# A Trainium2 encoder block: stacked parts in the low-rank factors, head norms on VectorE, and attention tables made inside the first feed-forward

## The chip, the core and the metric

The kernel runs on one core of a Trainium2 chip. That core has four compute engines with their own instruction queues: TensorE (PE, matrix products into PSUM), VectorE (DVE), ScalarE (ACT) and GpSimd (POOL). SyncE (SP) only issues DMAs, as ACT and POOL also can. Each engine works through its queue in order and waits on semaphores for the others. The metric is the device time of one execution in microseconds (us); lower is better.

## What is computed

Two layers on x of shape (1, 512, 1024), float32: an RWKV-7 time mixing with a SwiGLU feed-forward, then a differential attention with another. The parts that the change touches:

```
w = -softplus(-(w0 + tanh(xw @ w1) @ w2)) - 0.5        # w1: 1024x64, w2: 64x1024
a = sigmoid(a0 + (xa @ a1) @ a2)                       # a1: 1024x64, a2: 64x1024
g = sigmoid(xg @ g1) @ g2                              # g1: 1024x160, g2: 160x1024
...
y = (y - mean) * rsqrt(var + 64e-5)                    # per head of 64
y = y * lnx_w + lnx_b
y = y + sum(r * k * r_k) * v
x = x + (y * g) @ w_o
...
q = partial_rope(rms_norm(q, q_norm_g))                # likewise k, with k_norm_g
lam = exp(sum(lam_q1 * lam_k1)) - exp(sum(lam_q2 * lam_k2)) + lam_init
```

## The kernel before

Activations lie transposed: 1024 features as eight tiles of 128 partitions by 512 tokens. A product is kept near float32 by splitting both sides into a high part (a cast to fp32r, on ACT) and a low part (the rest, a subtraction on DVE) and adding three fp32r products (`mm3`, L156 to L158): high by high, low activation by high weight, high activation by low weight. The low-rank factors are the exception: `lora` and `lora2` (L384, L400) use plain fp32 tiles.

The RWKV layer comes first, to about 526 us. Its 16 heads are worked in two halves, w = 0 and 1. `lora` for w1 and a1 runs beside the first half of r; `rates` then makes w2 and a2 into the sigmoids for a half (four output tiles each, L400 with the sigmoid L493 as evacuation, four PSUM banks `pj`). Behind that `plan` merges three streams in an order fixed by the due times in `TIMES`: half 0 (`pairs`, `solve`, the recurrence `rec`), half 1 the same, and a stream of projections that ends with `gate` (the first factor g1, a sigmoid) and `out_half(0)`. `out_half` calls `lora2` with the two pieces of g2 (128 and 32 rows) and multiplies each result by the heads' output (evacuations L597, L601, L603), then projects with w_o, whose high and low parts are made at L617 and L618. `out_half(1)` comes after everything else, at the tail of the layer.

`head_out` normalizes one tile of 128 tokens and eight heads: mean and variance on DVE (L839 to L846, the square L843 on ACT), then `rsqrt`, whose first step is a power on POOL (L227) with three small DVE steps behind it (L229 to L231), the multiplication L853 on DVE, for each parity of heads the gain (L857) and the bonus times v (L858) on POOL, the sum L860 on DVE, and four transpositions on PE (L865), copied out on ACT (L866). It runs eight times, four for each half. `rsqrt_v` (L239 to L245) is a version that stays on DVE, used for the norms of the pairs.

The first feed-forward follows to 895 us, then the attention to 1166 us and the second feed-forward. Each begins with a norm of its input, `norm_cols`: squares on ACT (L267), their sums on POOL and DVE (L272, L274), a product with ones on PE (L281), then L283, the power L227 and L229 to L231; in the feed-forward also L253 and, on PE, L254. The attention's setup makes its tables there: a broadcast load of 192 KB (`lv`, L928) from ACT's queue, rotary tables with the norm gains (L935 to L945, DVE), and lambda (L947 to L951, with an exponential on ACT). The feed-forward's weights come through `load_w`: DMA, cast `wh` (L150, ACT), low part `wl` (L151, DVE). The gain tiles of the norm are `xa` and `xb` (L296 on ACT, L297 on DVE). The order of each engine's queue follows from the order of the code and from when buffers come free, as a scheduler decides it.

## Time and profile before

| | |
|---|---|
| median of three runs | 1536.3 us (1527.12 to 1544.98) |
| the profiled execution | 1535.6 us |
| its span, first to last instruction | 1533.8 us |
| PE busy | 1461.6 us, 95% |
| DVE, ACT, POOL busy | 766.8, 521.4, 210.7 us |

The span is what the rows' times count from; 1.8 us of the execution lie around it. A share of busy time is an average over stages with different limits. A row in the timeline names in brackets how long the engine was idle before it and what ended that. In the windows view the granted clock of TensorE is given as a share of the full 2.4 GHz; 0.50 is 1.2 GHz.

### The profile page before, as it was taken

How to read it: one execution, taken by the hardware profiler on the slowest of the kernel's cores; microseconds unless marked ns; L12 is line 12 of the kernel's file. 1: busy time of each engine (PE TensorE's matmuls, PEld its weight loads, DVE VectorE, ACT ScalarE, POOL GpSimd, SP SyncE). 2: the span in 40 equal slices, each digit the busy share in tenths (PEclk: the TensorE clock that was granted, in tenths of full speed). 3: DMA queues.
4: the chain of work that ended last, by engine and by line, in shares of the span. 5: the costliest groups of instructions: out<-in, count | busy, mean ns of one | idle time of the engine just before them, and what ended most of it. 6: DMA issues, size and time to landing. Idle time of an engine off the chain costs nothing.

```text
span 1533.8 us, 23005 instructions
## 1 busy us (share of the span) xinstructions
PE 1461.6 (95%) x9576; PEld 1133.6 (74%) x9576; DVE 766.8 (50%) x1420; ACT 521.4 (34%) x913; POOL 210.7 (14%) x180
## 2 busy tenths in 40 slices
PE   3899998999998999999999989999999999999999
PEld 2475655766585778888888879998778888888887
DVE  6645558586354644343423276666666444443222
ACT  4552241213212432222222153456654332222111
POOL 0013212112022111111100013211001111111000
PEclk9999999999699899999999999999999999999999
DMA  4022434756131222222222231211012222222231
GB/s 143 18 100 98 154 113 139 279 208 206 61 107 46 97 96 95 95 87 96 95 97 96 96 107 65 83 56 56 29 42 97 97 96 96 97 96 96 98 124 67
DMA packets 51801, 154.24 MB, mean 101 GB/s; under 512 B 5488, under 2 KB 12016, under 8 KB 49648
## 3 DMA queue, kind: packets, MB, share of 16 engines
q1 hardware_dynamic: 50496, 151.18, 28.8%
q8 instruction: 75, 1.23, 0.3%
q10 hardware_dynamic: 1120, 1.32, 0.3%
q14 instruction: 30, 0.25, 0.1%
q0 software_dynamic: 80, 0.26, 0.0%
HBM read 131.77 MB, written 20.97 MB: 100 GB/s over the span
## 4 chain that ended last, share of the span: by engine, by line
PE 82%; DVE 8%; ACT 3%; POOL 3%; issue 2%; DMA 1%; ACTq 0%; SPq 0%; POOLq 0%; DVEq 0%
PE pj L156 15%; PE pj L157 14%; PE pj L158 14%; PE pj L182 3%; PE pj L216 3%; PE d L1007 3%; PE d L1009 2%; PE d L1008 2%; PE cb L698 2%; PE ca L788 2%; PE cb L830 2%; POOL ty L227 2%; PE pj L400 2%; PE a L1105 1%; PE ca L158 1%
## 5 line engine op out<-in xcount | busy, mean ns | idle before, releaser
L150 ACT CAST wh<-wr 128x1024 fp32r<-128x1024 f32 x153 | 161.0, 1053 | 498.3 <-PE pj L157 224.4
L151 DVE TENSOR_TENSOR wl<-wr,wh 128x1024 fp32r<-128x1024 f32 x153 | 187.0, 1223 | 184.2 <-ACT wh L150 182.6
L156 PE MATMUL pj<-xa,wh 128*128 128x512 f32 x352 | 139.2, 395 | 1.3 <-ACT wh L150 1.3
L157 PE MATMUL pj<-xa,wh 128*128 128x512 f32 x352 | 138.9, 395 | 0.0
L158 PE MATMUL pj<-xa,wl 128*128 128x512 f32 x352 | 138.8, 395 | 0.0
L156 PE MATMUL pj<-xb,wh 128*128 128x512 f32 x352 | 137.1, 389 | 0.0
L158 PE MATMUL pj<-xb,wl 128*128 128x512 f32 x352 | 137.1, 389 | 0.0
L157 PE MATMUL pj<-xb,wh 128*128 128x512 f32 x352 | 136.9, 389 | 0.0
L897 POOL TENSOR_TENSOR hid<-ev,hid 128x512 fp32r<-128x512 f32 x44 | 68.2, 1549 | 403.6 <-ACT hid L896 403.6
L893 DVE TENSOR_TENSOR ev<-pj,bc 128x512 f32<-128x512 f32 x44 | 30.4, 691 | 144.1 <-PE pj L158 144.1
L227 POOL TENSOR_TENSOR ty<-ty,mhalf 128x8 f32<-128x8 f32 (+1 forms) x28 | 49.1, 1752 | 302.4 <-DVE ty L846 148.8
L890 DVE TENSOR_TENSOR ev<-pj,bc 128x512 f32<-128x512 f32 x44 | 30.4, 692 | 117.6 <-PE pj L158 115.0
L156 PEld LDWEIGHTS pj<-xa,wh 128*128 128x128 f32 x352 | 66.3, 188 | 17.4 <-ACT wh L150 2.2
L157 PEld LDWEIGHTS pj<-xa,wh 128*128 128x128 f32 x352 | 66.3, 188 | 15.5
L158 PEld LDWEIGHTS pj<-xa,wl 128*128 128x128 f32 x352 | 66.3, 188 | 15.5
L157 PEld LDWEIGHTS pj<-xb,wh 128*128 128x128 f32 x352 | 66.1, 188 | 13.8
L156 PEld LDWEIGHTS pj<-xb,wh 128*128 128x128 f32 x352 | 66.1, 188 | 13.6
L158 PEld LDWEIGHTS pj<-xb,wl 128*128 128x128 f32 x352 | 66.1, 188 | 13.6
L158 PE MATMUL pj<-hid,wl 128*128 128x512 f32 x176 | 68.5, 389 | 0.0
L156 PE MATMUL pj<-hid,wh 128*128 128x512 f32 x176 | 68.5, 389 | 0.0
L157 PE MATMUL pj<-hid,wh 128*128 128x512 f32 x176 | 68.5, 389 | 0.0
L216 PE MATMUL pj<-wr,xk 128*128 128x512 f32 x128 | 61.8, 622 | 0.0
(310 smaller groups left out, 3095.4 us busy)
## 6 DMA issues: line engine op xcount, KB each, us to landing
wr<-in_wgu SPq DMA_DIRECT2D x88, 512.0 KB, 3.5
wr<-in_wdn SPq DMA_DIRECT2D x44, 512.0 KB, 3.5
st_d<-z SPq DMA_DIRECT2D x16, 1024.0 KB, 4.7
z<-st_d SPq DMA_DIRECT2D x16, 1024.0 KB, 5.8
wr<-in_w_kv SPq DMA_DIRECT2D x16, 512.0 KB, 3.5
wr<-in_w_r SPq DMA_DIRECT2D x8, 512.0 KB, 3.4
wr<-in_w_k SPq DMA_DIRECT2D x8, 512.0 KB, 3.5
wr<-in_w_v SPq DMA_DIRECT2D x8, 512.0 KB, 3.5
```

The lines of the kernel that those rows point to most:

```text
L150: nc.scalar.copy(hi, raw)
L151: nc.vector.tensor_tensor(out=lo, in0=raw, in1=hi.bitcast(F32), op=ALU.subtract)
L156: mm(out, wh, xh, start=start, stop=False)
L157: mm(out, wh, xl, start=False, stop=False)
L158: mm(out, wl, xh, start=False, stop=stop)
L182: self.nc.tensor.matmul(pss[i], w[:, kt % 2, i * P:i * P + P], x, start=kt == kts[0], stop=kt == kts[-1])
L216: self.nc.tensor.matmul(pss[tt], x[:, tt * P:(tt + 1) * P], w[:, kt % 2, :], start=kt == 0, stop=kt == KT - 1)
L227: nc.gpsimd.tensor_tensor(out=y, in0=m, in1=half.to_broadcast(shp), op=ALU.pow)
L400: self.nc.tensor.matmul(ps, a[:, i * P:i * P + P], t[0:r], start=n == 0, stop=n == len(ws) - 1)
L698: nc.tensor.matmul(ps[f, o:o + P], BK[f, hf * 4 + c2 * 2 + c, u, :], Z[f, c2 * 2 + c, 0:2, :].rearrange("p a b -> p (a b)"), start=True, s ...
L897: nc.gpsimd.tensor_tensor(out=t[:, 1, :], in0=b, in1=t[:, 0, :].bitcast(F32), op=ALU.subtract)
L1007: mm(ps[:, t], x[:, 0, :], hi, start=kt == 0, stop=False)
```

## The change

Four things change.

1. The second low-rank factors are computed with fp32r products instead of fp32 ones. For w2 and a2 the weight is loaded twice, one copy under the other (128 rows), the activation is stored as its high part in rows 0 to 63 and its low part in rows 64 to 127, and one product of 128 rows does two of the three terms; a second, of 64 rows with the low weight, does the third. For this the first factor's weights are loaded side by side twice (`repeat`), so that its result comes out twice. For g2 the 128-row piece is split as elsewhere, and the 32-row piece is stacked three times (96 rows), so that each output takes four products.
2. In `head_out` the inverse root is `rsqrt_v` on DVE, the gain is multiplied on DVE, and the bonus multiplication on POOL is written ahead of the root.
3. The attention's tables move out of `attn` into `attn_setup`, called at the seventh column of the first feed-forward; `lv` and `lp` get a buffer of their own.
4. The first gate factor's last part gets 96 rows instead of 32.

```diff
@@ -53,12 +53,12 @@
...
-    LO = dict(rk="p", dc="p", z0="p", ka="p", bk="p", yf="d", yl="p", vt="p", su="d", sv="d")
-    AT = dict(lv=1, ah=2, al=2, kq=8, e=3, pt=2, hq=7, hu=2, sq=2, jk=1, h8=4)
+    LO = dict(rk="p", dc="p", z0="p", ka="p", bk="p", yf="d", yl="d", vt="p", su="d", sv="d")
+    AT = dict(ah=2, al=2, kq=8, e=3, pt=2, hq=7, hu=2, sq=2, jk=1, h8=4)
...
@@ -336,7 +336,7 @@
...
-                self.open(st, "hl", dict(wh=2, wl=2), reuse_waits="tile")
+                self.open(st, "hl", dict(wh=2, wl=2, lv=1, lp=1), reuse_waits="tile")
                 x = self.ffn(x, 0, "xa")
...
@@ -373,31 +373,66 @@
...
-    def lora(self, h, m, W1, act, dst, tag):
-        nc = self.nc
-        ws = [self.load_raw(w, [P, KT, w.shape[2]]) for w in W1]
+    def repeat(self, src, n):
+        r = src.shape[2]
+        t = self.T("wr", [P, KT, n * r])
+        for i in range(n):
+            self.nc.sync.dma_start(t[:, :, i * r:i * r + r], src)
+        return t
+    def lora(self, h, m, W1, out, tag):
+        nc = self.nc
+        ws = [self.repeat(w, n) for w, n in W1]
         pss = [self.bank(tag) for _ in W1]
         for kt in range(KT):
             x = self.mix_tile(h, m, kt)
             for ps, w in zip(pss, ws):
                 nc.tensor.matmul(ps[0:w.shape[-1], :], w[:, kt, :], x, start=kt == 0, stop=kt == KT - 1)
             yield
-        for w, ps, t in zip(ws, pss, dst()):
-            r = w.shape[-1]
-            if act is None:
-                nc.vector.tensor_copy(t[0:r], ps[0:r, :])
-            else:
-                nc.scalar.activation(t[0:r], ps[0:r, :], act)
-    def lora2(self, parts, W2, w, evac):
-        ws = [self.load_raw(a[:, w * 512:w * 512 + 512], [a.shape[0], 512]) for a in W2]
+        out(*pss)
+    def halves(self, dst, src):
+        nc = self.nc
+        nc.scalar.copy(dst, src)
+        nc.vector.tensor_tensor(out=dst[C:P], in0=src[C:P], in1=dst[C:P].bitcast(F32), op=ALU.subtract)
+    def lora2(self, x, W2, w, evac):
+        nc = self.nc
+        raw = self.T("wr", [P, 512])
+        for f in (slice(0, C), slice(C, P)):
+            nc.sync.dma_start(raw[f], W2[:, w * 512:w * 512 + 512])
+        hi, lo = self.T("ho", [P, 512], F32R), self.T("ho", [P, 512], F32R)
+        nc.scalar.copy(hi, raw)
+        nc.vector.tensor_tensor(out=lo[0:C], in0=raw[0:C], in1=hi[0:C].bitcast(F32), op=ALU.subtract)
         for i in range(4):
             ps = self.bank()
-            for n, (t, a) in enumerate(zip(parts, ws)):
-                r = a.shape[0]
-                self.nc.tensor.matmul(ps, a[:, i * P:i * P + P], t[0:r], start=n == 0, stop=n == len(ws) - 1)
+            c = slice(i * P, i * P + P)
+            nc.tensor.matmul(ps, hi[:, c], x, start=True, stop=False)
+            nc.tensor.matmul(ps, lo[0:C, c], x[0:C], start=False, stop=True)
+            evac(w * 4 + i, ps)
+    def gate2(self, pg, w, evac):
+        nc, A = self.nc, self.A
+        c0 = slice(w * 512, w * 512 + 512)
+        raw = self.load_raw(A["g2a"][:, c0], [P, 512])
+        hi, lo, st = (self.T("pr", [P, 512], F32R) for _ in range(3))
+        nc.scalar.copy(hi, raw)
+        nc.vector.tensor_tensor(out=lo, in0=raw, in1=hi.bitcast(F32), op=ALU.subtract)
+        raw = self.T("wr", [P, 512])
+        for i in range(3):
+            nc.sync.dma_start(raw[i * 32:i * 32 + 32], A["g2b"][:, c0])
+        nc.scalar.copy(st[0:96], raw[0:96])
+        nc.vector.tensor_tensor(out=st[32:64], in0=raw[32:64], in1=st[32:64].bitcast(F32), op=ALU.subtract)
+        for i in range(4):
+            ps = self.bank()
+            c = slice(i * P, i * P + P)
+            self.mm3(ps, hi[:, c], lo[:, c], pg[0], pg[1], True, False)
+            nc.tensor.matmul(ps, st[0:96, c], pg[2][0:96], start=False, stop=True)
             evac(w * 4 + i, ps)
     def rwkv(self, turn):
@@ -434,11 +469,15 @@
         pwa = []
         def low(i):
-            def dst():
-                pwa or pwa.append(self.T("s", [P, 2, S]))
-                return [pwa[0][:, i, :]]
-            return dst
-        self.merge(*zip((normed(), self.lora(h, 1, [A["w1"]], AF.Tanh, low(0), "ca"), self.lora(h, 4, [A["a1"]], None, low(1), "cb"), self.r_half(0)),
+            def out(ps):
+                pwa or pwa.append(self.T("s", [P, 2, S], F32R))
+                if i:
+                    return self.halves(pwa[0][:, 1, :], ps)
+                t = self.T("pr", [P, S])
+                nc.scalar.activation(t, ps, AF.Tanh)
+                self.halves(pwa[0][:, 0, :], t)
+            return out
+        self.merge(*zip((normed(), self.lora(h, 1, [(A["w1"], 2)], low(0), "ca"), self.lora(h, 4, [(A["a1"], 2)], low(1), "cb"), self.r_half(0)),
                         self.START))
         sg, aa = self.rates(pwa[0], 0)
         kr, ld, pg, sa, x1 = ([], []), ([], []), [], [(sg, aa)], []
@@ -479,18 +518,24 @@
         return mix
     def gate(self, pg):
-        def dst():
-            t = self.T("s", [P, 2, S])
-            pg.extend((t[:, 0, :], t[:, 1, :]))
-            return pg
-        return self.lora(self.h, 5, [self.A["g1a"], self.A["g1b"]], AF.Sigmoid, dst, "pj")
+        nc = self.nc
+        def out(a, b):
+            t, u = self.T("s", [P, 2, S], F32R), self.T("s", [P, 2, S], F32R)
+            pg.extend((t[:, 0, :], t[:, 1, :], u[:, 0, :]))
+            for ps, hi, lo, f, g in ((a, pg[0], pg[1], slice(0, P), slice(0, P)), (b, pg[2], pg[2], slice(0, 96), slice(64, 96))):
+                v = self.T("pr", [P, S])
+                nc.scalar.activation(v[f], ps[f], AF.Sigmoid)
+                nc.scalar.copy(hi[f], v[f])
+                nc.vector.tensor_tensor(out=lo[g], in0=v[g], in1=hi[g].bitcast(F32), op=ALU.subtract)
+        return self.lora(self.h, 5, [(self.A["g1a"], 1), (self.A["g1b"], 3)], out, "pj")
     def rates(self, low, w):
         nc, A = self.nc, self.A
         sg = [self.T("s", [P, 2, S]) for _ in range(2)]
         aa = [self.T("s", [P, 2, S]) for _ in range(2)]
         for i, W2, dst, b in ((0, A["w2"], sg, "w0"), (1, A["a2"], aa, "a0")):
-            self.lora2([low[:, i, :]], [W2], w, lambda o, ps: nc.scalar.activation(dst[o // 2 - 2 * w][:, o % 2, :], ps, AF.Sigmoid, bias=self.vec(b, o)))
+            self.lora2(low[:, i, :], W2, w, lambda o, ps: nc.scalar.activation(dst[o // 2 - 2 * w][:, o % 2, :], ps, AF.Sigmoid, bias=self.vec(b, o)))
         return sg, aa
     def r_half(self, w):
@@ -601,7 +646,7 @@
             nc.scalar.copy(h, yx[o])
             yl[o] = self.T("xk", [P, S], F32R)
             nc.vector.tensor_tensor(out=yl[o], in0=yx[o], in1=h.bitcast(F32), op=ALU.subtract)
-        self.lora2(pg, [A["g2a"], A["g2b"]], w, ev)
+        self.gate2(pg, w, ev)
         yield
         def add(o, ps):
@@ -845,17 +890,18 @@
...
         nc.vector.tensor_scalar(var, var, 1.0 / C, 64e-5, op0=ALU.mult, op1=ALU.add)
         yield
-        rs = self.tiny([P, 8])
-        self.rsqrt(rs, var)
         vt = self.T("ho", [P, 2, 4, C])
         for par in range(2):
             nc.sync.dma_start(vt[:, par], self.v_d[w, par, tt * P:(tt + 1) * P])
+        for par in range(2):
+            self.lo("vt").tensor_tensor(out=vt[:, par], in0=vt[:, par], in1=self.bon[:, tt, w4:w4 + 4, par:par + 1].to_broadcast([P, 4, C]), op=ALU.mult)
+        rs = self.tiny([P, 8])
+        self.rsqrt_v(rs, var, "ty")
         nc.vector.tensor_tensor(out=yf, in0=yf, in1=rs.unsqueeze(2).to_broadcast([P, 8, C]), op=ALU.mult)
         lv = self.lw[:, w * 512:w * 512 + 512].rearrange("p (a b c) -> p b a c", b=2, c=C)
         yo = sq.rearrange("p (a b) c -> p a b c", b=2)
         for par in range(2):
-            self.lo("yl").tensor_tensor(out=y[:, par], in0=y[:, par], in1=lv[:, par], op=ALU.mult)
-            self.lo("vt").tensor_tensor(out=vt[:, par], in0=vt[:, par], in1=self.bon[:, tt, w4:w4 + 4, par:par + 1].to_broadcast([P, 4, C]), op=ALU.mult)
+            nc.vector.tensor_tensor(out=y[:, par], in0=y[:, par], in1=lv[:, par], op=ALU.mult)
             nc.vector.tensor_tensor(out=yo[:, :, par, :], in0=y[:, par], in1=vt[:, par], op=ALU.add)
         yield
@@ -884,6 +930,8 @@
                 for kt in range(KT):
...
                 pss.append(ps)
+            if f == 6 and l == 0:
+                self.attn_setup()
             if f == 0:
                 nc.scalar.copy(bc, self.rows_bc(self.norm_cols(xT)))
             a = self.T("ev", [P, S])
@@ -918,11 +966,9 @@
...
-    def attn(self, xT):
+    def attn_setup(self):
         nc, A, cp = self.nc, self.A, self.cp
-        kqv = [[None] * 3 for _ in range(4)]
-        ins = self.heads_in(kqv, self.head_weights(A["w_q"][0], ("wh", "wl")))
-        self.xs = self.gain_split(xT, "g_mix1", "xa")
         lv = self.lv = self.T("lv", [P, 6, C])
         nc.scalar.dma_start(lv, A["hv"].unsqueeze(0).broadcast_to([P, 6, C]))
@@ -941,7 +987,7 @@
...
-        lp = self.T("hq", [P, 2, C])
+        lp = self.T("lp", [P, 2, C])
         nc.vector.tensor_tensor(out=lp, in0=lv[:, 0:4:2, :], in1=lv[:, 1:4:2, :], op=ALU.mult)
         ld = self.tiny([P, 2])
         nc.vector.tensor_reduce(out=ld, in_=lp, axis=AX.X, op=ALU.add)
@@ -959,6 +1005,11 @@
...
+    def attn(self, xT):
+        nc, A, cp = self.nc, self.A, self.cp
+        kqv = [[None] * 3 for _ in range(4)]
+        ins = self.heads_in(kqv, self.head_weights(A["w_q"][0], ("wh", "wl")))
+        self.xs = self.gain_split(xT, "g_mix1", "xa")
         st = self.STEPS
```

**The order of instructions at three places.** PE at the gate's second factor for the first half. `pj` are the PSUM banks, `s` the gate's activation, `wr` the g2 tiles; before, the fp32 products of lines L400 lie between transpositions (L865) and the solve (L760):

```order
L760 MATMUL cb_3214<-s_3123,s_3133 32x32 x3
L400 MATMUL pj_3309<-s_3294,wr_3305 128x512
L865 MATMUL cb_3111<-cst,ho_3089 128x128
L400 MATMUL pj_3309<-s_3294,wr_3307 128x512
L760 MATMUL cb_3249<-s_3123,s_3133 32x32 x32
L400 MATMUL pj_3318<-s_3294,wr_3305 128x512
L400 MATMUL pj_3318<-s_3294,wr_3307 128x512
L400 MATMUL pj_3326<-s_3294,wr_3305 128x512
```

And of the change, where `pr` are the split g2 tiles, L435 is the stacked product, L911 the transposition and L805 the solve:

```order
L156 MATMUL pj_3397<-s_3366,pr_3386 128x512
L157 MATMUL pj_3397<-s_3366,pr_3386 128x512
L911 MATMUL cb_3183<-cst,ho_3154 128x128
L156 MATMUL pj_3408<-s_3366,pr_3386 128x512
L158 MATMUL pj_3397<-s_3366,pr_3387 128x512
L157 MATMUL pj_3408<-s_3366,pr_3386 128x512
L158 MATMUL pj_3408<-s_3366,pr_3387 128x512
L156 MATMUL pj_3418<-s_3366,pr_3386 128x512
L805 MATMUL cb_3321<-s_3195,s_3205 32x32 x32
L435 MATMUL pj_3397<-s_3367,pr_3388 128x512
L435 MATMUL pj_3408<-s_3367,pr_3388 128x512
```

Two fp32 products for each bank became four fp32r ones, and two of the stacked ones now stand behind the solve's block.

DVE at the last head normalization, the tail of the RWKV layer (`ty` are the 8-column statistics, `ho` the heads' tile). Before:

```order
L846 TENSOR_SCALAR ty_4244<-ty_4244 128x8
L229 TENSOR_TENSOR ty_4250<-ty_4248 128x8
L230 SCALAR_TENSOR_TENSOR ty_4250<-ty_4250,ty_4244 128x8
L231 SCALAR_TENSOR_TENSOR ty_4247<-ty_4250,ty_4248 128x8
L853 TENSOR_TENSOR ho_3991<-ho_3991,ty_4247 128x512
L860 TENSOR_TENSOR ho_4242<-ho_3991,ho_4254 128x4x64 x2
```

And of the change (L891, L900 and L906 are the former L846, L853 and L860; steps L243 to L245 come three times, shown once):

```order
L891 TENSOR_SCALAR ty_4361<-ty_4361 128x8
L239 TENSOR_SCALAR ty_4370<-ty_4361 128x8
L240 TENSOR_SCALAR ty_4370<-ty_4370 128x8
L243 TENSOR_TENSOR ty_4373<-ty_4370 128x8
L244 SCALAR_TENSOR_TENSOR ty_4373<-ty_4373,ty_4361 128x8
L245 SCALAR_TENSOR_TENSOR ty_4370<-ty_4373,ty_4370 128x8
...
L900 TENSOR_TENSOR ho_4101<-ho_4101,ty_4369 128x512
L904 TENSOR_TENSOR ho_4101<-ho_4101,lw 128x256 x2
L906 TENSOR_TENSOR ho_4359<-ho_4101,ho_4364 128x4x64 x2
```

DVE goes through from the variance to the sum without a step of POOL between, but for the bonus tile, which POOL writes earlier.

DVE at the start of the attention, from the sum of squares (L274) to L283, which reads PE's L281 (`wl` and `al` are low parts of weights, `xb` gain tiles). Before, with the tables and four gain tiles already behind it:

```order
L274 TENSOR_TENSOR hq_6903<-hq_6903,hq_6905 128x512
L151 TENSOR_TENSOR wl_6978<-wr_6975,wh_6977 128x1024
L283 TENSOR_SCALAR ty_7005<-c_7000 128x4
L297 SCALAR_TENSOR_TENSOR xb_7028<-x_3301,par,xb_7028 128x512
L229 TENSOR_TENSOR ty_7010<-ty_7008 128x4
```

And of the change, where no gain tile stands ahead of it:

```order
L274 TENSOR_TENSOR hq_7044<-hq_7044,hq_7046 128x512
L151 TENSOR_TENSOR al_7125<-wr_7122,ah_7124 128x1024
L297 SCALAR_TENSOR_TENSOR xb_7157<-x_3376,par,xb_7157 128x512
L297 SCALAR_TENSOR_TENSOR xb_7160<-x_3376,par,xb_7160 128x512
L297 SCALAR_TENSOR_TENSOR xb_7163<-x_3378,par,xb_7163 128x512
L297 SCALAR_TENSOR_TENSOR xb_7166<-x_3378,par,xb_7166 128x512
L297 SCALAR_TENSOR_TENSOR xb_7169<-x_3380,par,xb_7169 128x512
L297 SCALAR_TENSOR_TENSOR xb_7172<-x_3380,par,xb_7172 128x512
L151 TENSOR_TENSOR wl_7119<-wr_7116,wh_7118 128x1024
L283 TENSOR_SCALAR ty_7146<-c_7141 128x4
```

The sum of squares moved ahead, and a low part and six gain tiles now stand between it and the low part that PE reads next. In the first feed-forward the table steps (L981 to L991, the former L935 to L945) stand directly ahead of that phase's L283 in DVE's queue.

## Rows read from the trace of the kernel before

**Rows 1.** The page of the profile: busy time by engine (share of the span, instructions), and the chain that ended last, by engine.
```profile
PE 1461.6 (95%) x9576; PEld 1133.6 (74%) x9576; DVE 766.8 (50%) x1420; ACT 521.4 (34%) x913; POOL 210.7 (14%) x180
...
PE 82%; DVE 8%; ACT 3%; POOL 3%; issue 2%; DMA 1%; ACTq 0%; SPq 0%; POOLq 0%; DVEq 0%
```

**Rows 2.** The windows view: for each stretch its length, the busy time (and instructions) of PE, PEld, DVE, ACT and POOL, the granted clock, the DMA share and GB/s. They lie at the gate's second factor, at the output projection behind it, in the recurrence of the first half, at the output projection of the second half, and at the first softmax of the attention.
```profile
390.00:395.00 5.00, 5.00 (x45) 2.02 (x45) 1.38 (x2) 1.26 (x4) 0.00 (x0) 0.54 0.00 0
...
409.90:414.30 4.40, 4.40 (x13) 3.47 (x11) 0.91 (x2) 1.05 (x1) 0.00 (x0) 0.50 0.28 104
...
330.00:340.00 10.00, 10.00 (x115) 5.83 (x115) 9.08 (x28) 0.95 (x2) 0.00 (x0) 1.00 0.36 136
...
500.00:506.40 6.40, 5.86 (x13) 4.30 (x14) 3.74 (x5) 2.06 (x3) 0.00 (x0) 0.50 0.25 79
...
980.00:990.00 10.00, 9.98 (x70) 7.53 (x70) 6.80 (x18) 6.02 (x21) 0.00 (x0) 1.00 0.34 105
```

**Rows 3.** PE between 388 and 420 us. The first row is the groups-by-line view of 388 to 409 us (busy us and mean ns of one; an fp32 product shows as two instructions, so x16 is eight products); the others are the timeline: start, length, line, operation, names, shape, count.
```profile
L400 PE MATMUL pj<-s,wr 128*128 128x512 f32 (+1 forms) x16 | 16.0, 1123 | 0.0
...
390.11 1.83 PE L400 MATMUL pj<-s,wr 128*128 128x512 f32 x2
...
409.94 0.79 PE L156 MATMUL pj<-s,s 128*128 128x512 f32 x1
...
414.34 0.40 PE L157 MATMUL pj<-xk,s 128*128 128x512 f32 x1
...
418.77 0.40 PE L156 MATMUL pj<-s,s 128*128 128x512 f32 x1
419.00 0.39 PE L157 MATMUL pj<-xk,s 128*128 128x512 f32 x1
```

**Rows 4.** The two `rates` stages, timelines of PE and ACT: the first at 77 to 84 us, the second at 203 to 211 us.
```profile
76.63 7.13 PE L400 MATMUL pj<-s,wr 64*128 64x512 f32 x16
84.09 1.09 PE L156 MATMUL pj<-z,z 128*128 128x512 f32 x3 [0.33 <-ACT z L199]
...
203.02 3.70 PE L400 MATMUL pj<-s,wr 64*128 64x512 f32 x8
...
210.59 3.70 PE L216 MATMUL pj<-wr,xk 128*128 128x512 f32 x8
...
205.94 3.73 ACT L493 ACTIVATE s<-pj,par 128x512 f32<-128x512 f32 x6
```

**Rows 5.** The waits of DVE between 260 and 500 us: the waiting line, what released it, us in total, times, the longest.
```profile
DVE ty L229 <- POOL ty L227: 9.8, 7, 1.8
...
DVE ho L860 <- POOL ho L858: 6.6, 4, 2.2
```

**Rows 6.** The last head normalization, timelines of DVE and PE at 479 to 501 us.
```profile
479.21 0.42 DVE L860 TENSOR_TENSOR ho<-ho,ho 128x256 f32<-128x256 f32 x1
...
487.00 0.17 DVE L846 TENSOR_SCALAR ty<-ty 128x8 f32<-128x8 f32 x1
...
490.29 0.69 DVE L853 TENSOR_TENSOR ho<-ho,ty 128x512 f32<-128x512 f32 x1
491.88 1.27 DVE L860 TENSOR_TENSOR ho<-ho,ho 128x256 f32<-128x256 f32 x2 [0.90 <-POOL ho L857]
...
480.77 1.12 PE L400 MATMUL pj<-s,wr 128*128 128x512 f32 x2
...
500.54 0.79 PE L156 MATMUL pj<-s,s 128*128 128x512 f32 x1 [4.00 <-ACT s L617]
```

**Rows 7.** The start of the first feed-forward, timelines of DVE and PE.
```profile
539.38 0.16 DVE L283 TENSOR_SCALAR ty<-cb 128x4 f32<-128x4 f32 x1 [1.29 <-PE cb L281]
...
542.63 1.16 PE L254 MATMUL cb<-ev,ones 128*128 128x128 f32 x8 [0.61 <-DVE ev L253]
```

**Rows 8.** The start of the attention, timelines of DVE, ACT and PE.
```profile
899.44 0.19 DVE L935 TENSOR_SCALAR lv<-lv 128x64 f32<-128x64 f32 x1
...
900.53 0.29 DVE L945 TENSOR_TENSOR hq<-lv 128x128 f32<-128x128 f32 x1
...
901.42 1.28 ACT L948 ACT_TABLE_LOAD   x1
...
901.60 2.07 DVE L297 SCALAR_TENSOR_TENSOR xb<-x,par,xb 128x512 fp32r<-128x512 f32 x3
...
902.72 0.21 ACT L948 ACTIVATE ty<-ty 128x2 f32<-128x2 f32 x1
...
897.80 2.56 ACT L296 ACTIVATE xb<-x,par 128x512 fp32r<-128x512 f32 x4
...
908.96 0.69 DVE L274 TENSOR_TENSOR hq<-hq,hq 128x512 f32<-128x512 f32 x1
909.56 1.22 DVE L151 TENSOR_TENSOR wl<-wr,wh 128x1024 fp32r<-128x1024 f32 x1
...
917.75 0.16 DVE L1043 TENSOR_SCALAR ty<-ty 128x8 f32<-128x8 f32 x1
...
922.61 1.12 PE L1065 MATMUL d<-cst,hq 128*128 128x128 f32 x4 [5.94 <-DVE hq L1056]
```

**Rows 9.** The DMA view: what was moved in the first 12 us, in 40 equal slices, and one issue at the attention's start (count, KB each, median us from issue to landing).
```profile
GB/s 0 0 0 0 0 0 75 34 198 244 341 413 387 398 389 396 389 389 335 335 396 423 414 410 408 414 414 426 398 420 444 389 410 396 328 177 280 300 376 416
...
lv<-in_hv ACTq DMA_DIRECT2D x1, 192.0 KB, 3.2
```

## The prediction

> **What bounds the kernel now.** I read the page first. PE is busy 95% of the span and carries 82% of the chain that ended last; DVE carries 8%, ACT 3%, POOL 3% [rows 1]. So an edit saves time only where it shortens PE's own work, where it shortens a stretch in which PE waits, or where PE runs at its lower clock. The profiled execution took 1535.6 us, 0.7 under the median of the runs shown (1536.3); the sum below is made against 1535.6.
>
> The windows show where the clock is low: around 390 to 414 us and 500 to 506 us the granted clock is 0.50 to 0.54, which is 1.2 instead of 2.4 GHz [rows 2]. In the first of these PE works on the gate's second factor, L400, 16.0 us for eight fp32 products; the output projection's first product starts at 409.94, and at 414.34 a product is down to 0.40 us: the clock is back [rows 3]. In the recurrence PE is full and DVE busy for 9.08 us of ten [rows 2]. At the tail PE waits for a chain over POOL and DVE [rows 6].
>
> **The change, part by part.**
>
> *First factors.* w1 and a1 are loaded twice, in pieces of 64 floats, to fill 128 rows; the product's moving size stays 512, so its time stays. The two w1 copies are issued while the x tiles still land and the DMA engines move about 400 GB/s [rows 9]. 256 KB is 0.65 us at that rate; if the small pieces went at half the rate, the two would take 1.3 more, and the norm behind the last x tile as well. Bounds 0 and +1.3, taken **+0.5**: the second copy only stands where a1's load of the same size stood. The Trainium skill, DMA: Bandwidth & Descriptors, "Why small descriptors are slow", counts 11 cycles for a 256-byte piece of which 8 carry data; by that, an estimate, the copies take 0.5 longer. No run here shows such a piece by itself.
>
> *rates, first half.* Eight fp32 products (7.13 us, [rows 4]) become sixteen fp32r ones. One takes 0.23 us at the full clock (418.77 to 419.00, [rows 3]), so 3.7 us. But they start about 2 us later (tanh, then a cast on ACT, then a subtraction on DVE of about 0.7 each), and then the sigmoids bound them: the table load 1.28 [rows 8] and eight of 0.62 (six in 3.73, [rows 4]), with four banks to write to. What is late next is L199's cast, for which PE waits at 84.09 [rows 4], since ACT has four casts more. Bounds 0 and +1.5, taken **+0.3**.
>
> *rates, second half.* PE spends 203.02 to 210.59, 7.6 us, where 3.7 would do [rows 4]; the splits of w2 and a2 hang on nothing new here. The sigmoids start at 205.94 [rows 4], so the fourth bank is free at 208.4 and PE's last product ends near 208.9: 1.7 less; without waits for banks it is 3.9. Bounds -3.9 and -0.5, taken **-2**.
>
> *Gate's second factor, first half.* Now 16 fp32r products: 3.7 us at full clock, 7.2 at half. Of the 19.8 us between 390.11 and 409.94 the other work takes 19.8 - 16.0 = 3.8 us, at the half clock [rows 3]. If the clock stayed at half until the projection begins, the stretch would be 7.2 + 3.8 = 11.0 us, 8.8 less; if it is back by then, the projection's 4.4 us at half clock [rows 2] become 2.2: -11.0. Where PE went over to dense fp32r work before, the clock came back 4.4 us after 409.94 [rows 3] and 5.9 us after 500.54 (506.40, [rows 2, 6]). If it comes back 4.4 us after the first product here, the stretch is 4.4 + (11.0 - 4.4)/2 = 7.7, 12.1 less, and with the 2.2 it is -14.3. If it stays at half until 414.3 whatever runs, the projection spends 13.2 instead of 4.4 us at half clock, and the gain is 8.8/2 = 4.4. I take **-12**, 2.3 short of the quick return, for the new casts and subtractions between the second sigmoid and the first product (one tile on ACT and one on DVE, 0.6 to 0.7 each, and the same again for the weights); bounds -14.3 and -4.4.
>
> *Head norms.* Per head POOL loses its power step and two gain multiplications; DVE gets eleven small steps instead of three, about 0.20 apart (0.17 each), and two multiplications of 0.42 [rows 6]: +2.45 us, 19.6 for eight heads. DVE waits 9.8 + 6.6 = 16.4 us for POOL in these places now [rows 5], so its calendar hardly changes, and PE has the other half's products meanwhile. Bounds -2 and +3 (a third of the 9.8 us which the first half's four heads add), taken **0**.
>
> *Tail.* There the chain is bare. From L846 at 487.00 to the end of L860 at 493.15 it takes 6.15 us [rows 6]. Now: 0.2 + 11 x 0.2 + 0.69 for L853 + 4 x 0.42 = 4.75, so -1.4. Ahead of it half an L400 product, 1.06 us from 480.77, becomes one fp32r product of 0.23: -0.8. Behind it the casts before 500.54 stay, and the low clock with them. Bounds -3 and -1, taken **-2.2**.
>
> *Tables made early.* In the first feed-forward the table steps stand in DVE's queue ahead of L283, which waits 1.29 us for PE, so DVE is free from 538.09 [rows 7]. They took 1.38 us in the attention (899.44 to 900.82, [rows 8]), so L283 comes at 539.47 instead of 539.38, and a reduction of 0.28 follows inside the chain: +0.4 at L254, where PE already waits. If the tables' DMA, 3.2 us from issue to landing [rows 9] and issued only behind the squares, lands late, L283 waits, and behind it all that L254 needs. Bounds +0.1 and +2.5, taken **+0.4**.
>
> In the attention ACT no longer does four gain tiles (2.56 us), a table load (1.28) and the split of ah ahead of the squares [rows 8], so L274 comes about 5 us earlier, at 904. But DVE then has a split of 1.2 and six gain tiles (three in 2.07) ahead of the weight split that PE needs: that ends at 904.6 + 1.2 + 4.0 + 1.2 = 911.0, where it ended at 910.78 [rows 8]. PE's first wait stays. In the chain behind it two gain tiles less stand ahead of L1043, 1.4 us, less what the split behind comes later: 0.8 off PE's wait of 5.94 us [rows 8]. Bounds -4 and 0, taken **-0.8**.
>
> The exponential's table has to be loaded again at the first softmax: 1.28 us on ACT [rows 8], where PE is busy 9.98 us of ten [rows 2]. Bounds 0 and +1.3, taken **+0.6**. The Trainium skill, ScalarE: Activation LUTs, "What ACT_TABLE_LOAD costs", adds a drain of 1.38 us to each switch, which would make that bound +2.7 and the sum 1.4 worse. The trace doesn't agree: the load at 901.42 takes 1.28, and the next activation starts at 902.72 [rows 8].
>
> Sum: 0.5 + 0.3 - 2 - 12 + 0 - 2.2 + 0.4 - 0.8 + 0.6 = -15.2; 1535.6 - 15.2 = 1520.4, so **1520 us**. All bounds at their best give -27, 1508; all at their worst +4, 1540.
>
> **Rivals.**
>
> *The clock stays low* through gate and projection, as before: 4.4 instead of 12, so 1528. For it: it was low for 24 us while PE was never idle [rows 2, 3]. Against it: both returns came 4 to 6 us into fp32r work.
>
> *The clock never falls at 390,* because PE is denser just before: 24.2 us at half clock become 3.7 + 1.9 + 2.2 = 7.8, a gain of 16.4; 1516, and 1513 if the attention's wait shrinks by 4.
>
> *Hidden:* the products wait for splits, loads or banks; the gate gives 5, the second rates nothing: 1529. The change then does to PE's work what it says and moves the time little.
>
> *Slower than before:* DVE becomes the bound of the recurrence, with 0.9 us of ten free at 330 to 340 [rows 2]. If each head's 2.45 us reached PE in full, +19.6 stands against -15.2: 1540. It decides from 1.9 us per head. Against it: the 16.4 us of waits that go.
>
> **How the numbers follow.** Forecast 0.55 (1514 to 1526), low clock 0.18, no fall 0.12, hidden 0.09, DVE bound 0.06. The range 1509 to 1532 leaves out the last and the tails of the others. One per cent, about what a measurement of this kernel can tell from no change, is 15.4 us: faster is below 1521. Somewhat over half of the forecast's chance and all of "no fall" lie below: 0.45. DVE bound with more on top: 0.05. The rest is within 1%: 0.50.
>
> **What would show it.** Right: a half-clock stretch near 390 under 10 us; gate's products there under 8 us; the rates stage near 203 under 6; L846 to L860 at the tail under 5; PE's second wait at the attention's start near 5. Wrong: a low clock beyond 400 us, PE waiting for DVE in the recurrence 4 us more than before, or DVE waiting for the tables' DMA near 538 us.

## The result, and the profile after

The changed kernel takes 1518.92 us (median of 9 runs, 1516.61 to 1524.30) against 1536.3 (median of 9 runs, 1526.05 to 1544.98): ratio 0.9895, 95% interval 0.9866 to 0.9924, so faster by about 1%. The forecast was 1520, with 1509 to 1532 as its range. The profiled execution took 1518.63 us, 17.0 less in its span than the one of before.

The page of the changed kernel, the lines that answer to [rows 1]:

```profile
PE 1447.9 (95%) x9576; PEld 1140.0 (75%) x9576; DVE 787.3 (52%) x1511; ACT 529.1 (35%) x926; POOL 187.3 (12%) x156
...
PE 83%; DVE 9%; ACT 3%; POOL 2%; issue 1%; DMA 1%; ACTq 0%; POOLq 0%
```

PE lost 13.7 us of busy time, work went from POOL to DVE (+20.5 us there, as the change says), and PE is still busy 95% of the span. Where the time went is read by taking the same instructions in both traces as marks and subtracting (before, after: the time from one mark to the next, us):

| stretch (marks by the line of before, in brackets of after; L272 and L254 are the same in both) | before | after | difference | predicted |
|---|---|---|---|---|
| start to the seventh L272 on DVE (x tiles landed) | 17.1 | 17.0 | -0.1 | +0.5 |
| to the first L646 (691) on DVE: first `rates` | 76.6 | 80.9 | **+4.3** | +0.3 |
| to the second L549 (594): second `rates` | 123.9 | 126.5 | **+2.6** | -2 |
| to the first L797 (842): up to the recurrence | 67.9 | 65.7 | -2.1 | none |
| to the ninth L797: recurrence, first half | 102.5 | 98.7 | **-3.8** | 0 |
| to the first output addition, L609 (654): the gate | 45.7 | 32.0 | **-13.7** | -12 |
| to the ninth addition: recurrence, second half, and tail | 79.0 | 75.6 | **-3.4** | -2.2 |
| to L254 of the first feed-forward | 30.0 | 30.1 | +0.1 | +0.4 |
| to L1065 (1116) in the attention | 380.0 | 378.8 | -1.2 | -0.8 |
| to the end, with the first softmax | 611.2 | 611.6 | +0.4 | +0.6 |

The sum is right, but not its parts: the two `rates` stages got slower where the prediction had them faster or even, and the head norms gave something where it had nothing. The two traces are single executions.

**rates.** PE's timeline of the first `rates` (start, length, names, shape, idle before); L414 is the product of 128 rows, L415 the one of 64:

```profile
77.45 0.51 PE L414 MATMUL pj<-s,ho 128*128 128x512 f32 x1 [2.01 <-DVE s L400]
77.89 0.49 PE L415 MATMUL pj<-s,ho 64*128 64x512 f32 x1
78.31 0.50 PE L414 MATMUL pj<-s,ho 128*128 128x512 f32 x1
...
81.12 0.80 PE L414 MATMUL pj<-s,ho 128*128 128x512 f32 x1
81.85 0.79 PE L415 MATMUL pj<-s,ho 64*128 64x512 f32 x1
...
86.91 0.79 PE L156 MATMUL pj<-z,z 128*128 128x512 f32 x1
```

The start times are what counts: 77.45, 77.89, 78.31 are 0.43 apart, where neighbouring products of this size stand 0.23 apart [rows 3]; from 81.12 on they are 0.72 apart. The sixteen take 9.46 us, more than the eight fp32 products before them (7.13, [rows 4]). The weight loads (PEld; LDWEIGHTS brings a product's stationary side into the array), same stretch, show why:

```profile
77.89 0.18 PEld L415 LDWEIGHTS pj<-s,ho 64*128 64x128 f32 x1 [0.25 <-issue]
78.31 0.19 PEld L414 LDWEIGHTS pj<-s,ho 128*128 128x128 f32 x1 [0.24 <-issue]
...
396.60 0.19 PEld L435 LDWEIGHTS pj<-s,pr 96*128 96x128 f32 x1
396.83 0.19 PEld L156 LDWEIGHTS pj<-s,pr 128*128 128x128 f32 x1
```

At 78.31 a load and its own product start together: the load doesn't run under the product ahead of it, and stands idle 0.24 us first. In the last two rows (the gate) the load at 396.60 serves the product that starts at 396.83 (below), under the one that runs. And the windows (PE, PEld, DVE, ACT, POOL busy, then the granted clock) show that the clock went down to 1.2 GHz in both stages (for 10.2 us from 80.55 on, and for 6.8 from 213.67):

```profile
80.50:85.00 4.50, 4.50 (x8) 1.88 (x7) 0.00 (x0) 2.62 (x4) 0.00 (x0) 0.51 0.28 108
85.00:90.00 5.00, 5.00 (x10) 3.08 (x11) 1.58 (x3) 3.67 (x6) 0.00 (x0) 0.50 0.00 0
213.50:217.50 4.00, 4.00 (x7) 1.50 (x7) 3.29 (x6) 2.05 (x3) 1.91 (x1) 0.52 0.00 0
```

**Gate.** Timeline of PE at the gate's second factor for the first half, and the windows over it:

```profile
391.18 0.80 PE L156 MATMUL pj<-s,pr 128*128 128x512 f32 x1 [0.18 <-ACT pr L424]
...
396.60 0.40 PE L158 MATMUL pj<-s,pr 128*128 128x512 f32 x1
396.83 0.40 PE L435 MATMUL pj<-s,pr 96*128 96x512 f32 x1
...
397.76 0.39 PE L435 MATMUL pj<-s,pr 96*128 96x512 f32 x1
```

```profile
390.00:392.00 2.00, 1.82 (x26) 1.33 (x27) 1.48 (x3) 1.81 (x6) 0.00 (x0) 0.79 0.20 64
392.00:394.00 2.00, 2.00 (x6) 1.51 (x6) 1.27 (x2) 0.75 (x2) 0.00 (x0) 0.50 0.00 0
394.00:396.00 2.00, 2.00 (x67) 1.33 (x67) 0.00 (x0) 0.10 (x1) 0.00 (x0) 0.86 0.63 240
396.00:400.00 4.00, 4.00 (x56) 3.03 (x57) 3.23 (x6) 1.72 (x3) 0.00 (x0) 1.00 0.05 15
```

The sixteen products and the solve between them take 391.18 to 397.99, and the clock is at half for 3.4 us instead of 23.9 (390.40 to 414.29 before).

**Tail.** DVE's timeline from the variance (L891, once L846) to the sum, as in [rows 6]:

```profile
472.41 0.17 DVE L891 TENSOR_SCALAR ty<-ty 128x8 f32<-128x8 f32 x1
...
476.24 0.75 DVE L906 TENSOR_TENSOR ho<-ho,ho 128x256 f32<-128x256 f32 x2
```

4.58 us to the end of L906 (4.75 predicted), without a wait for POOL; it was 6.15.

### The profile page after: what moved, and what is told of

It reads as the page before. It is cut to its first block, busy times and chain, and to the rows that moved or that the text cites. A ratio compares the mean times of both kernels' runs of the same rounds, so it can differ in the third digit from the quotient of the medians.

```text
span 1516.8 us, 23107 instructions
## 1 busy us (share of the span) xinstructions
PE 1447.9 (95%) x9576; PEld 1140.0 (75%) x9576; DVE 787.3 (52%) x1511; ACT 529.1 (35%) x926; POOL 187.3 (12%) x156
## 4 chain that ended last, share of the span: by engine, by line
PE 83%; DVE 9%; ACT 3%; POOL 2%; issue 1%; DMA 1%; ACTq 0%; POOLq 0%
PE pj L156 15%; PE pj L157 15%; PE pj L158 15%; PE pj L182 3%; PE pj L216 3%; PE d L1058 2%; PE cb L875 2%; PE d L1060 2%; PE d L1059 2%; PE ca L833 2%; PE cb L743 1%; PE a L1156 1%; PE ca L157 1%; PE cb L157 1%; PE ca L158 1%
## 5 line engine op out<-in xcount | busy, mean ns | idle before, releaser
L945 POOL TENSOR_TENSOR hid<-ev,hid 128x512 fp32r<-128x512 f32 x44 | 68.2, 1551 | 403.6 <-ACT hid L944 403.6
L156 PEld LDWEIGHTS pj<-xb,wh 128*128 128x128 f32 x352 | 66.1, 188 | 13.7
L227 POOL TENSOR_TENSOR ty<-ty,mhalf 128x8 f32<-128x8 f32 (+1 forms) x20 | 35.4, 1770 | 157.6 <-DVE ty L1094 125.7
```

Source lines behind the costliest of these rows:

```text
L156: mm(out, wh, xh, start=start, stop=False)
L227: nc.gpsimd.tensor_tensor(out=y, in0=m, in1=half.to_broadcast(shp), op=ALU.pow)
L945: nc.gpsimd.tensor_tensor(out=t[:, 1, :], in0=b, in1=t[:, 0, :].bitcast(F32), op=ALU.subtract)
```

## The experiments

The granted clock differs from run to run, so a median mixes two things. Every run has its span and its mean granted clock; (1 - clock) x span is what the low clock cost it, an estimate that takes the whole span as scaling with the clock, and span x clock is the rest. Averaged over each kernel's runs, in us (for before, twelve that ran beside e1; the experiments ran on three chips, and before's rest beside each group is 1508.3 to 1509.6):

| kernel | median us | ratio to before, 95% | rest | clock |
|---|---|---|---|---|
| before | 1536.3 | 1 | 1508.8 | 25.1 |
| after | 1518.92 | 0.9895 [0.9866, 0.9924] | 1492.6 | 25.1 |
| e1_full_rows | 1508.5 | 0.9804 [0.9741, 0.9867] | 1490.4 | 16.2 |
| e12_rows96 | 1508.66 | 0.9804 [0.9745, 0.9863] | 1491.2 | 15.4 |
| e2_grouped | 1522.91 | 0.9893 [0.9818, 0.9968] | 1493.4 | 27.4 |
| e6_rates_back | 1514.71 | 0.9845 [0.9783, 0.9907] | 1497.9 | 14.7 |
| e3_heads_back | 1533.69 | 0.9989 [0.9950, 1.0027] | 1499.2 | 32.0 |
| e7_heads_back2 (on e1) | 1517.26 | 0.9881 [0.9811, 0.9952] | 1495.4 | 20.5 |
| e10_power_back (on e1) | 1517.42 | 0.9881 [0.9795, 0.9967] | 1494.8 | 20.5 |
| e8_gate_back2 (on e1) | 1511.72 | 0.9845 [0.9776, 0.9914] | 1497.3 | 12.8 |
| e9_tables_back2 (on e1) | 1509.28 | 0.9827 [0.9757, 0.9896] | 1491.6 | 15.8 |
| e11_heads_gate_back (on e1) | 1534.05 | 0.9980 [0.9948, 1.0012] | 1499.7 | 32.5 |

In these means the change takes 16 us off the rest and nothing off the clock's cost. In the two traces the half clock is shorter by 20.5 us at the gate and longer by 17.1 in the two `rates` stages.

### The 64-row products of rates

e1 makes the third product 128 rows long as well (its lower half adds the product of the two low parts, which the kernel otherwise leaves out):

```diff
-        nc.vector.tensor_tensor(out=lo[0:C], in0=raw[0:C], in1=hi[0:C].bitcast(F32), op=ALU.subtract)
+        nc.vector.tensor_tensor(out=lo, in0=raw, in1=hi.bitcast(F32), op=ALU.subtract)
...
-            nc.tensor.matmul(ps, lo[0:C, c], x[0:C], start=False, stop=True)
+            nc.tensor.matmul(ps, lo[:, c], x, start=False, stop=True)
```

> The changed kernel with one edit: the third term's weight and activation take all 128 rows instead of the first 64, so that all sixteen products of a rates stage have the same rows (the added rows multiply the two low parts). Theory A (in the changed kernel a product of 64 rows stands between products of 128, and at each change the weight load of 0.19 us is no longer beside the product before it, so that a product takes 0.43 us instead of 0.23, and the clock falls behind that): spacing 0.23, no half clock between 80 and 90 us and between 213 and 222 us, rates of the first half 3 to 5 us shorter, the second 3 to 5 us, of which some is lost again as waits; 1511 to 1515 us. Theory B (the wait of 2 us ahead of the stage lets the clock fall, and banks and sigmoids set the spacing): spacing at least 0.4 on average, half clock again, 1517 to 1520 us.

Measured: 1508.5, Theory A, and 2.5 under its range. PE's timeline of the first `rates` in e1:

```profile
74.63 0.50 PE L414 MATMUL pj<-s,ho 128*128 128x512 f32 x1 [2.01 <-DVE s L400]
74.97 0.40 PE L415 MATMUL pj<-s,ho 128*128 128x512 f32 x1
75.21 0.39 PE L414 MATMUL pj<-s,ho 128*128 128x512 f32 x1
```

The wait ahead is the same 2.01 us, the spacing is 0.23, the sixteen take 4.83 us with 0.40 of a wait for a bank among it, and the clock stays at 2.4 GHz in both stages. The `rates` stretches of the table fall from 80.9 to 74.5 and from 126.5 to 119.9. More arithmetic, 10 us less; by the table 8.9 of it is the clock's. That the clock stays up isn't sure in each execution: behind the same wait of 2.0 us it stayed up in e1, e7, e9, e10 and e11 and fell for 3.4 us in e8 and e12. With 64 rows it fell in all three traces (after, e2, e3), for 10.2 to 13.7 us. In the second stage it fell in these three and in none of the seven.

e2 keeps the 64 rows and writes the products in groups: four of 128, then four of 64.

```diff
...
+        pss = [self.bank() for _ in range(4)]
+        for i, ps in enumerate(pss):
+            nc.tensor.matmul(ps, hi[:, i * P:i * P + P], x, start=True, stop=False)
+        for i, ps in enumerate(pss):
+            nc.tensor.matmul(ps, lo[0:C, i * P:i * P + P], x[0:C], start=False, stop=True)
```

> The changed kernel with one edit: in a rates stage the four products of 128 rows of a weight come first, then the four of 64 rows, instead of one of each in turn. Theory A1 (the change of the row count costs): only one product in four at 0.43 us, the others at 0.23; the stage 2 to 3 us shorter, 1514 to 1517 us. Theory A2 (a product of 64 rows cannot take its weight load beside the product before it, whatever that was): the products of 64 rows at 0.43, those of 128 at 0.23; a saving of 1 to 2 us. Theory B (banks and sigmoids): no difference.

Measured: 1522.91, no faster than after. The scheduler, which waits for banks, put half of the products back into alternation, so as a remedy it fails; but the groups that it left together tell what was asked. e2's timeline at the first and the second `rates` (L413 has 128 rows here):

```profile
79.74 2.07 PE L415 MATMUL pj<-s,ho 64*128 64x512 f32 x4
81.80 0.80 PE L413 MATMUL pj<-s,ho 128*128 128x512 f32 x1
...
209.40 0.73 PE L415 MATMUL pj<-s,ho 64*128 64x512 f32 x2
210.06 0.50 PE L413 MATMUL pj<-s,ho 128*128 128x512 f32 x1
210.49 0.73 PE L415 MATMUL pj<-s,ho 64*128 64x512 f32 x2
```

From 209.40 the pair takes 0.66 to the next product's start and that one 0.43, together 1.09 where three neighbours of 128 rows take 0.69: 0.40 for two changes, as in after, and nothing between 64 and 64. At half clock four of 64 rows take 2.06 (79.74 to 81.80), near 3 x 0.43 + 0.72 = 2.01. So it isn't 64 rows that cost, but going over. One reservation: the trace puts the load at 210.06 down to a bank that became free, so the change back to 128 rows isn't alone there.

e12 asks whether any change of the row count costs. It is e1 with `lo[0:96, c], x[0:96]` in the product.

> As e1_full_rows, but the third term of the rates products takes 96 rows (all low weight rows are made; the rows 64 to 95 add half of the product of the two low parts) instead of 64 (after) or 128 (e1). Theory A1 (any change of the row count between neighbouring products keeps the next weight load out of the running product): L414 and L415 stand 0.43 us apart, the clock falls in both rates stages, 1519 us as after. Rival A2 (only 64 rows and fewer put TensorE into another arrangement, and going over to it or back waits for the running product; 96 rows count as 128, as the L435 rows between 128-row products suggest): 0.23 us apart as in e1, no half clock in the rates, 1508 us.

Measured: 1508.66, as e1: Rival A2. Its first `rates`:

```profile
80.68 0.63 PE L414 MATMUL pj<-s,ho 128*128 128x512 f32 x1
81.10 0.63 PE L415 MATMUL pj<-s,ho 96*128 96x512 f32 x1
...
82.57 0.40 PE L415 MATMUL pj<-s,ho 96*128 96x512 f32 x1
82.80 0.40 PE L414 MATMUL pj<-s,ho 128*128 128x512 f32 x1
```

0.23 at the full clock, and 0.43 in this execution only for the 3.3 us at half clock, where it was 0.72 in after. So 96 rows go with 128, and 64 don't. This is what the Trainium skill says in TensorEngine Tiling (Array Packing), Tiling Modes, "Key Properties": changing the tiling mode drains the engine; its "Performance Considerations", "When to Use Tiling", name row tiling for a contraction of 64 and less. The trace fits that, though no view names a mode, and gives the price: 0.20 us per change at 2.4 GHz, 0.29 at 1.2 (0.72 - 0.43).

e6 puts the old fp32 products of `rates` back into after, with w1 and a1 loaded once.

```diff
...
-            self.lora2(low[:, i, :], W2, w, lambda o, ps: nc.scalar.activation(dst[o // 2 - 2 * w][:, o % 2, :], ps, AF.Sigmoid, bias=self.vec(b, o)))
+            self.lora2_f32([low[:, i, :]], [W2], w, lambda o, ps: nc.scalar.activation(dst[o // 2 - 2 * w][:, o % 2, :], ps, AF.Sigmoid, bias=self.vec(b, o)))
```

> The changed kernel with the two rates stages as before (fp32 products, first factors loaded once); the gate's factor stays changed. At 217 us it should be 6.8 us ahead of the changed kernel. Theory S (stages behind take delays up): at the end only 2 to 5 us of that are left, 1514 to 1517 us. Theory H (what the recurrence gave came from the head norms alone): all 6.8 left, 1512 us.

Measured: 1514.71, 4.2 under after, in Theory S's range: this part of the change, as it is written, costs more than it brings. By the table it saves 5.3 of the rest and loses 10.4 to the clock. But e6's recurrence of the first half takes 98.9 us, as after's 98.7: that gain isn't delay from `rates` made up, as Theory S had it.

### The head norms

e3 puts the root and the multiplications of `head_out` back on POOL, in after; e7 does so in e1:

```diff
...
+        rs = self.tiny([P, 8])
+        self.rsqrt(rs, var)
...
-        self.rsqrt_v(rs, var, "ty")
...
+            self.lo("yl").tensor_tensor(out=y[:, par], in0=y[:, par], in1=lv[:, par], op=ALU.mult)
+            self.lo("vt").tensor_tensor(out=vt[:, par], in0=vt[:, par], in1=self.bon[:, tt, w4:w4 + 4, par:par + 1].to_broadcast([P, 4, C]), op=ALU.mult)
```

> The changed kernel with the head norms as they were before: power on POOL, gain on POOL, the bonus multiplication behind it. Theory H (the 6 us that the recurrence of the first half gave, between 231 and 388 us, come from POOL steps that DVE and PE no longer wait for): 4 to 6 us of them gone, and 1.5 us at the tail; 1524 to 1528 us. Theory S (they are delay from the rates that the stages behind had waits to take up): only the tail's 1.5 us and 1 us in the second half, 1520 to 1522 us.

> e1_full_rows with the head norms as before (e3's edit without the half clock of the rates stages, so that only the heads differ). Theory H (the head norms on DVE give 7 us: about 5 in the recurrence of the first half, 2 in the second half and at the tail): 1515 to 1517 us, up to 300 us level with e1. Theory C (e3's loss was mostly half clock that came by chance of the execution): 1510 to 1512 us.

e10 puts only the root back (`rsqrt` for `rsqrt_v`), in e1.

> e1_full_rows with only the power step back on POOL (the gain stays on DVE, the bonus multiplication stays early). Theory P (the wait for the power step is what the heads gave): 4 to 6 of the 7 us gone, 1512 to 1515 us. Theory M (the two gain multiplications on POOL and the wait for them are it): 1 to 2 us gone, 1509 to 1511 us.

Measured: 1533.69 (14.8 over after), 1517.26 (8.8 over e1) and 1517.42 (8.9 over e1); the first and the last lie above the ranges of both their theories, the second just above Theory H's. By the table 6.6, 5.0 and 4.4 of these are in the rest and 6.9, 4.3 and 4.3 in the clock. The recurrence's first half takes 102.5 us before and 102.1, 105.3 and 102.9 in e3, e7 and e10, against 98.7 in after and 98.5 in e1 (e7's holds 6.8 us at half clock, from 319.5 on, which the others don't have). PE's waits in it: before; in after and in e1, the same line; e7; e10 (the line that waits, what released it, us, times, the longest):

```profile
PE ca L788 <- DVE rs L818: 2.1, 2, 1.1
PE ca L802 <- DVE rs L797: 0.8, 2, 0.5
PE pj L384 <- DVE xm L373: 0.5, 1, 0.5
PE ca L788 <- DVE rs L807: 0.4, 1, 0.4
```

```profile
PE ca L833 <- DVE rs L852: 0.4, 1, 0.4
```

```profile
PE ca L833 <- DVE rs L863: 2.2, 2, 1.1
PE pj L392 <- DVE xm L373: 1.0, 1, 1.0
PE ca L847 <- DVE rs L842: 0.9, 2, 0.5
PE ca L833 <- DVE rs L852: 0.4, 1, 0.4
```

```profile
PE pj L392 <- DVE xm L373: 1.8, 1, 1.8
PE ca L833 <- DVE rs L863: 1.1, 1, 1.1
PE ca L833 <- DVE rs L852: 1.0, 2, 0.6
```

PE waits for DVE 3.8 us before, 0.4 in after and e1, 4.5 in e7 and 3.9 in e10; the 3.4 from before to after are nearly the whole difference of 3.8. DVE itself waits for POOL's root (L229 for L227) 4.8 us before and in e7 and 5.0 in e10, and not at all in e1. So the head norms were no neutral exchange: DVE's queue is in order, and a wait in it for POOL delays what PE waits for. By the medians the root alone makes the whole of it; with four runs each, spread over 4 and 7 us, a share of 2 us for the gain multiplications can't be ruled out.

### The gate and the clock

e8 has the gate's fp32 products back, in e1:

```diff
...
-        self.gate2(pg, w, ev)
+        self.lora2_f32(pg, [A["g2a"], A["g2b"]], w, ev)
```

> e1_full_rows with the gate's second factor as before, eight fp32 products for each half. Theory G (fp32 products there let the clock stay at half, fp32r ones bring it back): 15 us or more of half clock from 375 us on, L400 at 14 to 16 us, 1519 to 1523 us. Theory G2 (the clock fell there because PE was thin ahead of it, and the heads on DVE have made it denser): no long half clock, the products 7 us, 1512 to 1514 us.

e11 has the gate and the head norms back, in e1 (the edits of e7 and e8 together).

> e1_full_rows with both the head norms and the gate's second factor as before; with e1, e7 and e8 it makes a table of two by two. Alone, the heads as before cost 8.8 us and the gate as before 3.2. If the two add (theory Add), 1520 to 1522 us, and the stretch from the last recurrence load of the first half to the first output addition takes 36 to 38 us (31.5 with both changed). If the clock is what they share (theory X: either one alone keeps the half clock short, only fp32 products behind a thin stretch leave it low for 20 us), more than the sum: 1525 to 1530 us, that stretch 43 to 46 us, 20 us or more of half clock in it.

Measured: 1511.72, with no long half clock at the gate, as Theory G2 had it, and 1534.05, as Theory X but 4 over its range. The fp32 products of the first half by line (busy us, mean ns of one), in e8 and then in e11:

```profile
L425 PE MATMUL pj<-s,wr 128*128 128x512 f32 (+1 forms) x16 | 8.6, 636 | 0.0
```

```profile
L425 PE MATMUL pj<-s,wr 128*128 128x512 f32 (+1 forms) x16 | 16.2, 1139 | 0.0
```

And the windows, in e8 and then in e11:

```profile
385.00:395.00 10.00, 10.00 (x116) 5.10 (x115) 7.24 (x11) 4.17 (x7) 0.00 (x0) 1.00 0.18 59
```

```profile
380.00:385.00 5.00, 3.79 (x82) 2.52 (x80) 1.58 (x3) 1.32 (x4) 1.83 (x4) 0.85 0.60 211
385.00:395.00 10.00, 10.00 (x80) 4.27 (x79) 2.76 (x4) 2.48 (x5) 0.00 (x0) 0.50 0.01 2
395.00:405.00 10.00, 10.00 (x30) 3.25 (x31) 4.25 (x6) 2.80 (x4) 0.00 (x0) 0.50 0.04 6
```

The same products run at 2.4 GHz in e8 and at 1.2 in e11. What differs is what stands ahead: in e11, as before, PE waits 1.2 us for the head's sum and is busy 3.79 us of five, the clock falls, and while the fp32 products run it stays down for 23.9 us; in e8 PE waits 0.1 us between 370 and 390. With the new products behind a PE that waits the clock falls as well, but for less: 10.2 us in e7, where PE waits 1.4 for the sum, and 3.4 in after and e1, where it still waits 1.8. In e6, which has the same wait of 1.8, it didn't fall at all. So the wait makes a fall likely and not certain, and the products decide how long it lasts.

The stretch of the table from the recurrence to the first output addition takes 45.6 us in e11 (45.7 before), 34.9 in e7, 33.8 in e8 and 31.5 in e1: either edit alone takes most of it, so the 24 us of half clock have two causes that need each other. In the medians, added to e1, the old gate costs 3.2 us, the old heads 8.8, both 25.5, not 12.0; by the table the excess is the clock's (12.8 in e8, 20.5 in e7 and 32.5 in e11, against 16.2 in e1), over runs whose mean clocks hardly meet (0.991 to 0.992 in e8, 0.983 to 0.989 in e7, 0.974 to 0.983 in e11). Not all of that lies at the gate of the first half. e11's second half and tail take 85.5 us, where e1 has 75.4 and before 79.0, with 30.7 us at half clock under the second half's fp32 products and behind them (13.7 in the tail of before).

### The tables

e9 calls `attn_setup` in the attention again, in e1 (`lv` and `lp` keep their new buffers).

```diff
-            if f == 6 and l == 0:
-                self.attn_setup()
...
+        self.attn_setup()
```

> e1_full_rows with the attention's tables made in the attention again. By the prediction's terms +0.4 in the first feed-forward, -0.8 and +0.6 in the attention: 0 to 1 us slower, 1508 to 1510 us. Rival (the first wait of the attention's start ends earlier with the change, against the prediction): 2 to 4 us slower, 1510 to 1513 us.

Measured: 1509.28 against 1508.5. This doesn't test where the tables are made, for they didn't move. e9's DVE in the first feed-forward, where L979 is the tables' first step:

```profile
510.04 0.19 DVE L979 TENSOR_SCALAR lv<-lv 128x64 f32<-128x64 f32 x1
...
511.40 0.16 DVE L283 TENSOR_SCALAR ty<-cb 128x4 f32<-128x4 f32 x1
```

They stand ahead of this phase's L283, as with the change: the scheduler made them as early, though the call stands in the attention. What the edit left in place is the buffer that `lv` and `lp` have of their own; that this buffer brings the tables forward wasn't tried.

So what the early tables are worth stays open. PE's waits from the first feed-forward to the attention's marked product, in after:

```profile
PE d L1059 <- DVE wl L151: 3.2, 2, 2.4
PE d L1116 <- DVE hq L1107: 3.1, 1, 3.1
```

Before, the second was 5.94 [rows 8] and those ahead of it 1.8 (L281) and 0.8 (a weight). The second is 2.8 shorter, and PE waits longer for weights ahead of it. The stretch is 1.2 us shorter than before; e7 and e12, with the same code there, take 379.7, so not even that is clear of the scatter.

## Why the prediction was right, point by point

- **Start** (+0.5): -0.1. This can't confirm or refute the term: with the same loads the mark comes at 14.6 to 17.5 us in the other traces.
- **rates, first half** (+0.3) **and second** (-2): +4.3 and +2.6. The step that failed is "One takes 0.23 us at the full clock (418.77 to 419.00, [rows 3]), so 3.7 us". That spacing is one between products of 128 rows; in alternation with 64 rows it is 0.43. The late start by 2 us was seen (2.01), but not that the clock would go down behind it. The second stage's products take 8.7 us (207.02 to 217.49, less 1.81 of other work), where under 6 was named. With e1's 128 rows the two stretches are 2.1 and 4.0 under before, some 2 better than forecast each.
- **Gate** (-12): -13.7. The product times and the quick return of the clock came as forecast (3.4 us at half clock; the chosen case had 4.4). But the clock's part isn't the products' alone: e8 shows that without them the clock would hardly have suffered once the head norms are on DVE. Of the 14 us that lie between e11 and e1 at the gate, either edit alone takes 11 to 12.
- **Head norms** (0): -3.8 in the recurrence. The step that failed is the end of its sentence on DVE's waits, "and PE has the other half's products meanwhile": PE waited 3.8 us for DVE there before, and 0.4 with the change. DVE's busy time rose as worked out. The rival that makes DVE the bound had the sign wrong.
- **Tail** (-2.2): -3.4 for it and the second half's recurrence; the chain itself is 4.58 for 4.75. The half clock there stayed (13.7 us in both), as said.
- **Tables** (+0.4, -0.8, +0.6): +0.1, -1.2 and +0.4 in their stretches. PE's second wait came out at 3.1 where near 5 was named, against longer waits ahead of it. No run isolates any of these terms.
- The 2.1 us between the second `rates` and the recurrence weren't forecast. That stretch takes 65.7 to 68.9 us in the eleven traces with the change or parts of it, and after's is the lowest, so this is within what single executions spread.

So the forecast was right in the main on its largest term, the gate, but that the sum came to 1520 is luck: two errors of `rates` (+8.6) stood against the head norms (-3.8), the gate (-1.7), the tail (-1.2), the stretch ahead of the recurrence (-2.1) and smaller ones (-1.5). With `rates` as forecast the kernel would have come out 8.6 lower, near 1510, at the lower end of the range, and e1 is below it.

## What to carry to other kernels

A product of 64 rows between products of 128 pays for two changes: fill it to 96 or 128 rows with a term that is otherwise dropped (1518.9 became 1508.7 and 1508.5 here; zeros weren't tried). On an engine whose queue is in order, moving a step to it is cheap if that takes a wait for another engine out of the queue, even where its busy time rises. A stretch at the low clock is to be costed together with the wait that stands ahead of it: here, taking away either the wait or the fp32 products was worth most of what both were. Compare mean clocks of several runs, since one trace shows one execution. And look in the trace whether an edit moved what it was to move: e9's didn't.

## What the runs showed of the hardware

- Going from 128 rows to 64 or back puts 0.20 us (0.29 at 1.2 GHz) between two 512-column products: the next weight load (0.18) starts with its own product (77.89 and 78.31 in after) and not under the one before. 96 rows don't do that (0.23 in e12).
- The unchanged kernel's runs on one chip spread from 1523.96 to 1545.18 us, and the mean granted clock goes with it: 0.991 in the first, 0.976 in the second. Span x clock is 1509 and 1506 us. Nearly all the spread is the clock's.
- fp32 products don't by themselves lower the clock: sixteen records of them took 8.6 us at 2.4 GHz in e8, where PE had waited 0.1 us ahead, and 16.2 at 1.2 GHz in e11, where it had waited 1.2. Once down at the gate, the clock came back after 3.4 us (after, e1) to 10.2 (e7) under fp32r products and after 23.9 under fp32 ones (before, e11).
